# A bidirectional encoder layer with a Fourier and a Hyena branch: the weight rooms' pool laid out first, token 512's product in banks T for the later Fourier halves, its column parts on GpSimd

## The chip, the cores and the metric

The kernel runs on one core of one Trainium2 chip. The metric is the device time of one execution in microseconds (us). One core has a matrix engine (TensorE, PE in the profile, with its weight loads as PEld), VectorE (DVE), ScalarE (ACT), GpSimd (POOL) and SyncE (SP), which issues most transfers. The engines run side by side, each takes its own instructions strictly in order, and they wait for one another by semaphores. Working data lies in SBUF (on-chip memory of 128 partitions), products of TensorE in PSUM banks.

## What is computed

Two sequences (`x_prompt`, `x_sample`, below b = 0 and 1) of 1024 tokens and 1024 channels pass through the same layer. Cut to what matters:

```
xn = rmsnorm(x, g_pre);  p = xn @ w_in                      # 1024 -> 8192 columns
fv, fg, hv, hg, mg = split(p)
fz  = fftn(fv.reshape(B, L, 4, 256), axes=(1, 3), norm="ortho").real
y_f = (fz * silu(fg)) @ w_fourier_out                       # Fourier branch
v, x1, x2 = split(short_conv(hv, w_short), 3)
kf  = hyena_filters(...)                                    # 2 orders, two-sided, rfft
z = v;  for n, gate in enumerate((x1, x2)): z = gate * long_conv(z, kf[:, n], hyena_d[n])
y_h = (z * silu(hg)) @ w_hyena_out                          # Hyena branch
g_f, g_h = split(sigmoid(mg + b_merge))
out = x + rmsnorm((g_f * y_f + g_h * y_h) @ w_out, g_post)
```

The transforms are done as matrix products.

## The kernel before

**Values in two parts.** TensorE works on a rounded float32. Each operand is therefore kept as a high and a low part (`split`, line 168): a cast makes the high part (on ScalarE at line 171, on another engine at 173), a subtraction makes the low part (line 181). `mm3` multiplies high by high, high by low and low by high.

**Fourier phase** (`phase_fourier`). For each b, `norm` and then `xtile` for eight channel tiles k: TensorE transposes and scales the tile (`tpx`), ScalarE copies it to `xg`, and sums and differences of token j and token 1024 - j (`eo`: tokens folded around the middle) are split into `eh` and `el`, which lie in the pool `fe`. Token 512 is its own mirror and doesn't fit into the folds; it goes as a column of its own, split into two pieces of 128 x 2 in `x5`. Then come two halves of the channel groups, four in all, in the order (b, half) = (0,0), (0,1), (1,1), (1,0); weights are folded ahead of them on VectorE and GpSimd. In a half (`fourier_half`):

- `pfv`: the folded tokens by the weights, for the even folds (e = 0, 260 columns, into `ee`) and the odd ones (e = 1, into `oo`).
- `pfx`: the column of token 512 by the same weights, a product of 36 x 260 in sixteen matmuls. ScalarE copies it to `x5t` (line 416), VectorE makes its low part.
- `stage`: transforms along the tokens, `pse` and `pso`. In each `pse` of the even folds one matmul adds the alternating signs times `x5t`. ScalarE copies `pse` out (`sev`, line 439), VectorE joins it with `pso`.
- `pP` and `pQ`: transforms along the channels; VectorE makes `fA` and `fB`, which GpSimd's queue stores to `d_fz` (lines 491 and 492).

**PSUM.** Three tags share the eight banks: "mm" (four: `pfv`, `pin`, and `tpx` of b = 1), "X" (two: `pP`, `pQ`, half of the stages, and `pfx`) and "T" (two: `tpx` of b = 0, the other half of the stages, and `pft` of the filters).

**Main phase** (`phase_main`). First come sixteen filters. `filter_taps` makes products `pft`, exponentials on ScalarE (line 652, behind a table load) and norms `pn`; `filter_spectrum` makes the transform `pXf`. Thirty gate tiles (`spill_gate`, each an in-projection `inproj` of 48 `pin` matmuls) are spread among the filters as fill. Then `branches` and `phase_blocks` follow, which the change doesn't touch.

**Weight rooms.** A weight half comes in as `wr` (line 769); ScalarE casts it to its high part (773) and writes the negative of that (774), and a GpSimd transfer adds the source onto the negative, which leaves the low part (775). `rooms` gives such a pair of parts four places in turn: two buffers of `wh`/`wl` in the pool `wp`, the tile `draw` in `cp`, and the tile `draw2` in `stage2`, which is the pool m2 of `phase_main`. In `draw` and `draw2` both parts together are called `whl`.

**What sets the order.** The Tile scheduler orders the instructions of each engine by a simulated timeline, so that a change of buffers can also move instructions. Pools are laid out in SBUF in the order in which they are opened. With `reuse_waits="tile"`, a tile of a new pool waits only for the earlier tiles that lay in the same place. The Fourier phase opened px, fw, fe, fc, ff; in their place now come wp and xp, and above these the five pools of `phase_main`. Before the change m2 comes last of the five, and `draw2` lies over tiles of ff, the pool that the Fourier halves work in until their last instruction.

Of the kernel before, what the change touches and what calls it, by code (L numbers as in the profile page):

```python
# [161 lines left out]
class K:  # L162
# [171 lines left out]
    def xtile(self, b, k, px, fo):  # L334


        nc, a = self.nc, self.a
        if b == 0:
            xk = lambda m: self.xs[m][:, k * P:(k + 1) * P]
        else:  # L340
            xt = px.tile([P, 8, P], F32, tag="x", name=f"xk{b}_{k}", bufs=3)
            nc.sync.dma_start(xt, a[f"x{b}"].rearrange("(m p) c -> p m c", p=P)[:, :, k * P:(k + 1) * P])
            xk = lambda m: xt[:, m]
        xg = px.tile([P, L + 2], F32, tag="xg", name=f"xg{b}_{k}", bufs=2)
        nc.gpsimd.memset(xg[:, L:L + 2], 0.0)
        for n in range(2):
            tp = self.psum("mm", 4, "tpx") if b else self.psum("T", 2, "tpx")
            for q in range(4):
                m = 4 * n + q
                self.mm(tp[:, q * P:(q + 1) * P], xk(m), self.diag[:, m], True, True)  # L350
            nc.scalar.activation(xg[:, 512 * n:512 * n + 512], tp, AF.Copy, scale=self.gpre[:, k:k + 1])
        self.stored = nc.sync.dma_start(self.d_x[b][k], xg[:, 0:L])
        eo = px.tile([P, 2, 2, 256], F32, tag="eo", name="eo", bufs=2)
        fw = xg[:, 0:512].rearrange("p (a r) -> p r a", r=2)
        bw = xg[:, 1024:512:-1].rearrange("p (a r) -> p r a", r=2)
        self.add("dve", eo[:, 0], fw, bw)
        self.sub("pool" if b else "dve", eo[:, 1], fw, bw)
        self.split(fo["eh"][:, k], fo["el"][:, k], eo, "dve", "act")
        x5 = fo["x5"][:, k]
        mid = xg[:, 512:513].to_broadcast([P, 2])  # L360
        self.split(x5[:, b:b + 33:32], x5[:, 2 + b:35 + b:32], mid, "dve" if b else "pool", "dve" if b else "pool")


    def open_weights(self, pw):
# [26 lines left out]
    def fourier_half(self, b, half, W, fo, px, pf, begun={}):  # L391
# [7 lines left out]
        for e, (W_, n, X_) in enumerate(((WE, 260, EE), (WO, 256, OO))):  # L399
            for m in range(4):  # L400
                p = begun.get((e, m))
                if p is None:
                    p = self.psum("mm", 4, f"pfv{e}")
                    for k in range(8):
                        self.pfv(p, e, m, k, W, fo)
                self.split(X_[0][:, m], X_[1][:, m], p[:, :n], "dve", "act")
                if e == (b + half == 0):

                    if m == 0:
                        p5 = self.psum("X", 2, "pfx")[0:36, :260]  # L410
                    for k in (2 * m, 2 * m + 1):
                        for i in range(2):
                            self.mm(p5, fo["x5"][:, k], WE[i][:, k], k + i == 0, k + i == 8)
# [499 lines left out]
    def phase_main(self, nct=8, nb=NB, nf=16):  # L913
        tc, nc, a = self.tc, self.nc, self.a
        with ExitStack() as es:
            pool = lambda n: es.enter_context(tc.tile_pool(name=n, bufs=1, reuse_waits="tile"))
            mf, wa, wb, mi = pool("mf"), pool("wa"), pool("wb"), pool("mi")
            self.stage2 = pool("m2")
            self.turn, self.unsaved = 3, []
            ws = Rooms(wa, wb)  # L920
            self.load_x(0, range(4))
            self.hid = ws.tile([P, L], F32R, tag="q", name="hid", bufs=2)
            hid = ws.tile([P, L], F32, tag="q", name="hidr", bufs=2)
            nc.sync.dma_start(hid, self.d_h)
            nc.scalar.copy(self.hid, hid)
            self.sub("dve", self.hid[64:128], hid[64:128], self.hid[64:128])
            taps = self.filter_taps(0, 0, ws)
            self.load_x(0, range(4, 8))
            self.cfw0 = mf.tile([P, 4 * P], F32, name="cfw0")
            self.cfwd = mf.tile([P, 2, 12 * P], F32R, name="cfwd")  # L930
            nc.sync.dma_start(self.cfw0, a["c_fw0"])
            nc.gpsimd.tensor_copy(self.cfwd[:, 0, 0:1], self.xl[4][:, 0:1])
            nc.gpsimd.dma_start(self.cfwd, a["c_fwd"])
            for t, n in ((self.th, "c_th"), (self.wsh, "w_short"), (self.bm, "b_merge")):
                nc.sync.dma_start(t, a[n])
            plain = [(5, c) for c in range(8)] + [(6, c) for c in range(8)] + [(4, c) for c in range(NH)]
            fill = sorted([((2 * c + 1) / len(plain), t) for c, t in enumerate(plain)]
                          + [((2 * c + 1) / max(NF, 1), (0, c)) for c in range(NF)])
            fill = [t for _, t in fill]
            for i in range(nf):  # L940
                nxt = self.filter_taps((i + 1) % 2, (i + 1) // 2, ws) if i + 1 < nf else None
                gates = fill[i * len(fill) // nf:(i + 1) * len(fill) // nf]
                if i < nf - 1:
                    self.filter_spectrum(i % 2, i // 2, taps, ws)
                for sec, c in gates:
                    self.spill_gate(0, sec, c, ws)
                if i == nf - 1:
                    first = [self.conv(1 + n, 0, ws, "vx"[n], 0, True) for n in range(2)]
                    self.filter_spectrum(i % 2, i // 2, taps, ws)
                taps = nxt  # L950
                if i == 4:
                    self.cinv = mi.tile([P, 2, INVW], F32R, name="cinv")
                if 4 <= i < 12:
                    w = slice((i - 4) * INVW // 8, (i - 3) * INVW // 8)
                    with tc.issue_after(self.added.ins):
                        nc.gpsimd.dma_start(self.cinv[:, :, w], a["c_inv"][:, :, w])
            self.branches(nb, nct, ws, *first)
# [576 lines left out]
```

## Time and profile before

| what | value |
|---|---|
| median of 3 runs | 2417.44 us (2414.99 to 2423.45) |
| profiled execution | 2422.64 us |
| its span in the trace | 2420.8 us |
| mean granted TensorE clock | 0.993 |

Roughly, the Fourier phase takes the first 250 us and the filters with their fill last until about 660 us. "Busy" counts an instruction from its start to its end, and a matmul's end is modelled. A row of the timeline has a start, a duration, the engine, the line of the kernel, output and inputs by name, shape, the number of instructions that the row joins, and in brackets how long the engine stood idle ahead of it and what ended that.

### The profile page before, as it was taken

How to read it: one execution, taken by the hardware profiler on the slowest of the kernel's cores; microseconds unless marked ns; L12 is line 12 of the kernel's file. 1: busy time of each engine (PE TensorE's matmuls, PEld its weight loads, DVE VectorE, ACT ScalarE, POOL GpSimd, SP SyncE). 2: the span in 40 equal slices, each digit the busy share in tenths (PEclk: the TensorE clock that was granted, in tenths of full speed). 3: DMA queues.
4: the chain of work that ended last, by engine and by line, in shares of the span. 5: the costliest groups of instructions: out<-in, count | busy, mean ns of one | idle time of the engine just before them, and what ended most of it. 6: DMA issues, size and time to landing. Idle time of an engine off the chain costs nothing. (4 is left out here: it accounts for less than half of the span.)

```text
span 2420.8 us, 37131 instructions
## 1 busy us (share of the span) xinstructions
PE 2360.9 (98%) x13006; PEld 2050.1 (85%) x13006; DVE 1978.2 (82%) x3744; ACT 1147.2 (47%) x2140; POOL 460.4 (19%) x595
## 2 busy tenths in 40 slices
PE   7999899999999999999999999999999999999998
PEld 6998788888888888888888888888878888888786
DVE  7786888888638999999899999997666687777787
ACT  6546666667544444444223222333344465656543
POOL 3331111111132232321034444310000000101000
PEclk9999999999999999999999999999999999999999
DMA  7737687787788777665365666553546688888744
GB/s 250 231 105 233 178 226 214 212 227 214 193 234 246 222 222 210 187 182 191 126 208 174 219 210 205 175 178 122 204 165 226 214 290 262 261 272 234 214 158 155
DMA packets 265426, 499.37 MB, mean 206 GB/s; under 512 B 26694, under 2 KB 92455, under 8 KB 265112
## 3 DMA queue, kind: packets, MB, share of 16 engines
q1 hardware_dynamic: 220092, 380.27, 47.9%
q0 software_dynamic: 44960, 116.72, 18.9%
q8 instruction: 102, 1.67, 0.3%
q14 instruction: 84, 0.69, 0.1%
q10 hardware_dynamic: 188, 0.02, 0.0%
HBM read 333.59 MB, written 167.51 MB: 207 GB/s over the span
## 5 line engine op out<-in xcount | busy, mean ns | idle before, releaser
L194 PE MATMUL pin<-xh,wh 128*128 128x512 f32 x1024 | 400.9, 392 | 0.3 <-DMA wh<-d_w 0.3
L194 PE MATMUL pin<-xl,wh 128*128 128x512 f32 x1024 | 401.1, 392 | 0.0
L194 PE MATMUL pin<-xh,wl 128*128 128x512 f32 x1024 | 399.8, 392 | 1.3 <-DMA wl<-d_w 1.3
L194 PE MATMUL pin<-xh,whl 128*128 128x512 f32 x896 | 291.2, 396 | 8.1 <-DMA whl<-in_w_in 4.5
L194 PEld LDWEIGHTS pin<-xh,wl 128*128 128x128 f32 x1024 | 192.7, 188 | 37.4 <-DMA wl<-d_w 1.7
L194 PEld LDWEIGHTS pin<-xh,wh 128*128 128x128 f32 x1024 | 192.8, 189 | 35.7 <-DMA wh<-d_w 0.8
L194 PEld LDWEIGHTS pin<-xl,wh 128*128 128x128 f32 x1024 | 192.7, 188 | 34.7
L194 PEld LDWEIGHTS pin<-xh,whl 128*128 128x128 f32 x896 | 167.2, 189 | 42.1 <-DMA whl<-in_w_in 5.2
L194 PE MATMUL pT<-cinv,yh 128*128 128x256 f32 x1024 | 192.9, 283 | 2.3 <-ACT yh L171 2.3
L194 PE MATMUL pin<-xl,whl 128*128 128x512 f32 x448 | 177.6, 397 | 0.0
L194 PEld LDWEIGHTS pT<-cinv,yh 128*128 128x128 f32 x1024 | 165.4, 191 | 12.5 <-ACT yh L171 2.8
L194 PE MATMUL pX<-bh,cfwd 128*128 128x256 f32 x768 | 159.4, 287 | 1.0 <-ACT bh L171 1.0
L181 DVE TENSOR_TENSOR t<-pX,k 128x1024 f32<-128x1024 f32 x128 | 155.3, 1213 | 3.8 <-PE pX L194 3.0
L171 ACT CAST yh<-y 128x512 fp32r<-128x512 f32 x128 | 79.3, 620 | 160.2 <-DVE y L181 122.6
L194 PE MATMUL pT<-cinv,yl 128*128 128x256 f32 x512 | 145.6, 284 | 0.0
L171 ACT CAST bh<-b 128x512 fp32r<-128x512 f32 x144 | 89.0, 619 | 100.5 <-DVE b L181 61.6
L194 PEld LDWEIGHTS pX<-bh,cfwd 128*128 128x128 f32 x768 | 126.1, 192 | 4.7 <-ACT bh L171 1.4
L181 POOL TENSOR_TENSOR draw<-draw 128x256 f32<-128x256 f32 x96 | 90.3, 940 | 114.1 <-DMA draw<-in_w_out 41.6
L194 PE MATMUL pX<-bl,cfwd 128*128 128x256 f32 x384 | 110.0, 286 | 1.2 <-DVE bl L181 1.2
L181 DVE TENSOR_TENSOR bl<-b,bh 128x512 fp32r<-128x512 f32 x144 | 100.0, 700 | 12.7 <-ACT bh L171 12.5
L181 DVE TENSOR_TENSOR yl<-y,yh 128x512 fp32r<-128x512 f32 x128 | 92.4, 722 | 13.9 <-ACT yh L171 13.7
L177 DVE SCALAR_TENSOR_TENSOR x<-pin,wsh,x 128x512 f32<-128x512 f32 (+1 forms) x128 | 90.3, 739 | 12.0 <-ACT x L795 11.9
(372 smaller groups left out, 6049.6 us busy)
## 6 DMA issues: line engine op xcount, KB each, us to landing
k<-d_k SPq DMA_DIRECT2D x128, 512.0 KB, 4.5
wr<-in_w_in SPq DMA_DIRECT2D x136, 256.0 KB, 3.5
d_g<-gt SPq DMA_DIRECT2D x92, 256.0 KB, 3.2
d_k<-kt SPq DMA_DIRECT2D x128, 128.0 KB, 3.7
d_k<-kt SPq DMA_DIRECT2D x64, 256.0 KB, 3.8
fz<-d_g SPq DMA_DIRECT2D x64, 256.0 KB, 5.2
wl<-in_w_in POOLq DMA_DIRECT2D x56, 256.0 KB, 5.3
whl<-in_w_in POOLq DMA_DIRECT2D x56, 256.0 KB, 5.5
```

What stands on the lines that cost most here:

```text
L171: self.rounded = nc.scalar.copy(h, src)
L177: self.nc.vector.scalar_tensor_tensor(out, a, s, b, op0=op0, op1=op1)
L181: return e.tensor_tensor(out, a, b, op=op)
L194: return self.nc.tensor.matmul(out, lhsT, rhs, start=start, stop=stop, skip_group_check=shared)
```

## The change

It has three parts.

```diff
@@ xtile
         mid = xg[:, 512:513].to_broadcast([P, 2])
-        self.split(x5[:, b:b + 33:32], x5[:, 2 + b:35 + b:32], mid, "dve" if b else "pool", "dve" if b else "pool")
+        self.split(x5[:, b:b + 33:32], x5[:, 2 + b:35 + b:32], mid, "pool", "pool")
@@ fourier_half
                 if e == (b + half == 0):
 
                     if m == 0:
-                        p5 = self.psum("X", 2, "pfx")[0:36, :260]
+                        p5 = self.psum("T" if e == 0 else "X", 2, "pfx")[0:36, :260]
@@ phase_main
-            mf, wa, wb, mi = pool("mf"), pool("wa"), pool("wb"), pool("mi")
             self.stage2 = pool("m2")
+            wa, mf, wb, mi = pool("wa"), pool("mf"), pool("wb"), pool("mi")
```

- The two pieces of token 512 are made by GpSimd for b = 1 as well; for b = 0 GpSimd made them already.
- `pfx` runs with the even folds in all halves but the first, where it runs with the odd ones. In those three halves it now takes a bank of "T"; in the first it keeps one of "X".
- m2 is opened first, so that `draw2` lies just above wp and xp, where `el` lay in fe. wa comes next, and mf, with two constant tables of the transform (`cfw0`, `cfwd`), behind it.

TensorE's order is the same up to about 90 us and from about 660 us on. Between them it changes at these places, and the other engines' orders with it.

**TensorE, end of the last half** (`pQ` of the half's last products ahead, then the stages `pse` and `pso` of the even folds). Before:

```order
L194 MATMUL pQ<-px,chx 128x256
L194 MATMUL pfx<-we_2407,x_278 36x260
L194 MATMUL pfx<-we_2408,x_278 36x260
...
L194 MATMUL pse<-seq,ee_2491 128x258 x2
L194 MATMUL pse<-seq,ee_2492 128x258
L194 MATMUL pse<-seq,ee_2491 128x258 x2
L194 MATMUL pse<-seq,ee_2492 128x258
L194 MATMUL pse<-alt,x5t 128x258 x2
L194 MATMUL pso<-seq,ee_2491 128x258 x2
```

After:

```order
L194 MATMUL pQ<-px,chx 128x256
L194 MATMUL pfv_2701<-wo_2409,el 128x256
L194 MATMUL pse<-seq,ee_2491 128x258 x2
L194 MATMUL pse<-seq,ee_2492 128x258
L194 MATMUL pse<-seq,ee_2491 128x258 x2
L194 MATMUL pse<-seq,ee_2492 128x258
L194 MATMUL pse<-alt,x5t 128x258
L194 MATMUL pso<-seq,ee_2491 128x258 x2
```

The sixteen matmuls of `pfx` have left the place between `pQ` and `pse`; they now stand some 120 to 150 rows earlier, among the `pfv` of this half. The second `pse` of the even folds follows after the first `pso`. The two halves before it change in the same way.

**ScalarE, the same stretch** (`oo` and `pfv` belong to the last half; `hid`, `w3s`, `dec` and `ex` to the first filter; `whl_3590` is a weight half in the room `draw2`). Before:

```order
L171 CAST oo0_2493<-pfv1_2701 128x256
L925 CAST hid_2991<-hidr_2992 128x1024
L171 CAST w3s_2999<-w3_2996 128x256
L641 ACTIVATE dec_3002<-dec_3002 128x256
L416 CAST x5t_279<-pfx_2522 36x260
L652 ACT_TABLE_LOAD
L652 ACTIVATE ex_3009<-dec_3002,vec_68 128x256 x2
L652 ACTIVATE ex_3019<-dec_3002,vec_68 128x256 x2
L439 COPY sev_2753<-pse_2738 128x258
```

After:

```order
L171 CAST oo0_2493<-pfv1_2701 128x256
L773 CAST whl_3590<-wr_3591 128x512
L439 COPY sev_2753<-pse_2738 128x258
L774 ACTIVATE whl_3590<-whl_3590 128x512
L439 COPY sev_2778<-pse_2763 128x258
L171 CAST xh0_0_2971<-xl0_0_2972 128x1024
L171 CAST pp0_2736<-sst_2754 128x514
```

The cast of `whl_3590` stood 57 rows further down, among the exponentials of the second filter; it now follows the last `oo`, and its transfer (line 775) on GpSimd's queue has moved from behind the last four `d_fz` stores to ahead of them. The table load and the exponentials follow after four casts of the loaded sequence and all four `sev` copies of the even folds and the first odd one. On SyncE's queue the first loads of the sequence (`xl`) now come ahead of `hidr`, `w3` and `dec`.

**GpSimd, the token stage of b = 1** (`eo` is the difference of the folds for tile k, `x5` the pieces of token 512, `d_fz0` the stores of the half before). Before:

```order
L491 DMA d_fz0_0_93<-fA_1012 128x1024
L492 DMA d_fz0_1_94<-fB_1013 128x1024
L181 TENSOR_TENSOR eo_1750<-xg1_0_1735 128x512
L181 TENSOR_TENSOR eo_1774<-xg1_1_1759 128x512
L491 DMA d_fz0_2_95<-fA_1080 128x1024
L492 DMA d_fz0_3_96<-fB_1081 128x1024
```

After:

```order
L181 TENSOR_TENSOR eo_1750<-xg1_0_1735 128x512
L173 CAST x5_278<-xg1_0_1735 128x2
L181 TENSOR_TENSOR x5_278<-xg1_0_1735,x5_278 128x2
L491 DMA d_fz0_2_95<-fA_1080 128x1024
L492 DMA d_fz0_3_96<-fB_1081 128x1024
L345 MEMSET xg1_2_1783 128x2
L181 TENSOR_TENSOR eo_1774<-xg1_1_1759 128x512
L173 CAST x5_278<-xg1_1_1759 128x2
L181 TENSOR_TENSOR x5_278<-xg1_1_1759,x5_278 128x2
```

Each `eo` is now followed by the two instructions that make token 512's pieces, sixteen in all, which have left VectorE. On TensorE the `pfx` of the half that follows asks for the pieces of six of the eight tiles ahead of the first `pfv` of that half.

Between the filters the `pin` matmuls of the fill stand further ahead: TensorE reaches a filter's `pXf` after some 12 to 20 us more of such work than before, and after the same amount again at the last filter.

## The prediction

> **What bounds the kernel now.** I read the page first, then the list of TensorE's waits, then a table by stage, and then the timeline at the places that these three point to. The page:
>
> ```profile
> span 2420.8 us, 37131 instructions
> PE 2360.9 (98%) x13006; PEld 2050.1 (85%) x13006; DVE 1978.2 (82%) x3744; ACT 1147.2 (47%) x2140; POOL 460.4 (19%) x595
> ```
>
> TensorE is busy for 2360.9 of 2420.8 us, so all its idle time together is 60 us. A change that leaves its matmuls alone can gain only from those 60 us, and from stretches where it is busy at a lower granted clock. The change touches nothing before about 90 us and nothing after about 660 us. There, the table by stage (window, length, then busy time of TensorE, its weight loads, VectorE, ScalarE and GpSimd, the granted clock, the DMA share and GB/s):
>
> ```profile
> 97.50:130.60 33.10, 30.46 (x249) 29.99 (x248) 27.14 (x58) 19.77 (x33) 14.24 (x16) 0.95 0.74 247
> 197.20:212.20 15.00, 10.29 (x65) 8.70 (x64) 8.80 (x21) 9.00 (x16) 1.06 (x2) 0.89 0.81 282
> 249.65:269.16 19.51, 9.97 (x39) 7.50 (x37) 17.36 (x40) 9.56 (x20) 3.67 (x5) 0.74 0.60 159
> 300.00:360.00 60.00, 60.00 (x341) 52.55 (x340) 53.23 (x127) 42.57 (x93) 6.64 (x8) 1.00 0.83 225
> 540.00:600.00 60.00, 60.00 (x330) 52.06 (x329) 50.70 (x126) 41.15 (x89) 7.79 (x10) 1.00 0.82 228
> 600.00:660.00 60.00, 60.00 (x317) 51.51 (x317) 43.17 (x103) 35.60 (x76) 7.37 (x9) 1.00 0.72 191
> ```
>
> From 300 us TensorE never rests. The first three windows are the ones with something to win: 2.6, 4.7 and 9.5 us idle, at clocks of 0.95, 0.89 and 0.74. The waits between 180 and 300 us say what ends those idle times (line waited for, sum, times, longest):
>
> ```profile
> PE pin L194 <- DMA whl<-in_w_in: 4.5, 1, 4.5
> PE pin L194 <- ACT whl L773: 3.6, 1, 3.6
> PE pse L194 <- DVE x5t L181: 2.0, 1, 2.0
> PE pse L194 <- ACT sev L439: 1.6, 1, 1.6
> ```
>
> The upper two belong to the weight rooms, the lower two to token 512's product. Both are what the change moves.
>
> **Term A, the fourth weight room.** TensorE's timeline:
>
> ```profile
> 249.65 1.11 PE L194 MATMUL pft<-w3s,hid 128*128 128x256 f32 x8
> 252.16 0.74 PE L194 MATMUL pft<-w3s,hid 128*128 128x256 f32 x4 [1.40 <-DVE T L181]
> 256.51 0.79 PE L194 MATMUL pin<-xh,whl 128*128 128x512 f32 x1 [3.61 <-ACT whl L773]
> 257.10 0.63 PE L194 MATMUL pin<-xl,whl 128*128 128x512 f32 x1
> 257.53 0.63 PE L194 MATMUL pin<-xh,whl 128*128 128x512 f32 x1
> 263.11 1.22 PE L194 MATMUL pin<-xh,whl 128*128 128x512 f32 x2 [4.52 <-DMA whl<-in_w_in]
> 269.16 0.38 PE L664 MATMUL pn<-acc,ones 128*128 128x128 f32 x2
> 290.09 0.40 PE L194 MATMUL pin<-xl,wh 128*128 128x512 f32 x1
> ...
> 296.01 0.39 PE L194 MATMUL pin<-xh,wh 128*128 128x512 f32 x1
> ```
>
> From 249.65 to 269.16 lie 19.5 us. In them stand 12 pft and 24 pins. A pin takes 0.228 us (the last two rows stand 26 pins apart: 5.92 us over 26), so 24 take 5.5 us; 12 pft at about 0.118 (the slope in the first row: eight that end 1.11 us after they began, the last of them 0.28 long) take 1.4. That is 7.0 us of work and 12.5 us of loss: 9.5 us idle, and some 3 us in which the matmuls run slowly after the gap (257.10 to 257.53 is 0.43 us for one pin, against 0.228).
>
> Why the wait: the room draw2 lies over ff, which the last Fourier instruction still uses. ScalarE's cast into it came at 255.86, and the accumulating transfer behind it landed only before 263.11:
>
> ```profile
> 255.86 0.60 ACT L773 CAST whl<-wr 128x512 fp32r<-128x512 f32 x1
> 258.97 0.89 POOL L775 DMA_DIRECT2D whl<-in_w_in  x1 [6.50 <-ACT whl L774]
> whl<-in_w_in POOLq DMA_DIRECT2D x6, 256.0 KB, 5.0
> ```
>
> Laid out first, draw2 lies over el, whose last reader is a pfv matmul just ahead of the first pse (before 197.19 us in the trace of before). In the new order the cast stands some 60 rows earlier on ScalarE, right behind the last oo cast; the transfer, 5.0 us from issue to landing, can then be there some 40 us before TensorE asks for it. I take 12.5 less the 1.40 us wait for VectorE's T, which nothing here touches: **-11.1 us**. The ends are -8.1 (only 3.61 + 4.52 go, and the clock dips all the same, through another gap) and -12.5. The next room in turn becomes the tightest. In the order it has its transfer issued ahead of its first pin by the work of more than one gate, so I put no new wait there; term D holds that doubt.
>
> **Term B, token 512's product.** The end of the last Fourier half:
>
> ```profile
> 197.19 0.64 PE L194 MATMUL pse<-seq,ee 128*128 128x258 f32 x4
> 199.66 0.62 PE L194 MATMUL pQ<-qp,chan 128*128 128x256 f32 x3 [1.12 <-DVE fB L177]
> 200.48 2.07 PE L194 MATMUL pfx<-we,x 128*36 128x260 f32 x16
> 205.52 0.51 PE L194 MATMUL pse<-alt,x5t 128*128 128x258 f32 x2 [2.01 <-DVE x5t L181]
> 208.34 1.50 PE L194 MATMUL pse<-seq,ex 128*34 128x258 f32 x6 [1.58 <-ACT sev L439]
> 205.03 1.28 ACT L652 ACT_TABLE_LOAD   x1
> 206.32 1.70 ACT L652 ACTIVATE ex<-dec,vec 128x256 f32<-128x256 f32 x4
> 207.93 0.35 ACT L439 COPY sev<-pse 128x258 f32<-128x258 f32 x1
> ```
>
> pfx sits between pQ and pse, and its result must pass ScalarE and VectorE before the alternating product of pse can run: 2.01 us of nothing. The sev copy then stands behind a table load and four exponentials, 1.28 + 1.70 us: 1.58 us more. The window of 15.0 us holds 65 matmuls by the table, 4 of them pins: 61 at 0.12 (pfx's sixteen end 2.07 us after they began) and 4 at 0.228 are 8.2 us; 6.8 are lost. In the new order pfx stands inside the pfv pass, tens of matmuls ahead, and the sev copies come ahead of the table load. The 1.12 us wait for VectorE's fB is not of this part and stays: -6.8 + 1.1 = **-5.7 us**, ends -3.6 (2.01 + 1.58) and -6.8.
>
> The two other halves that change place have the same form, but with pfv, tpx and pse matmuls around them; their waits are part of term C.
>
> **Term C, the token stage of b=1.** The eight pairs of column pieces go from VectorE to GpSimd. What they cost on either engine (b=1 on VectorE between 100 and 140 us; b=0 on GpSimd between 20 and 60), and what GpSimd has there already:
>
> ```profile
> L173 DVE CAST x<-xg 128x2 fp32r<-128x2 f32 x8 | 5.2, 667 | 0.0
> L181 DVE TENSOR_TENSOR x<-xg,x 128x2 fp32r<-128x2 f32 x8 | 2.4, 316 | 0.1
> L173 POOL CAST x<-xg 128x2 fp32r<-128x2 f32 x8 | 9.1, 1136 | 13.0 <-ACT xg L351 13.0
> L181 POOL TENSOR_TENSOR x<-xg,x 128x2 fp32r<-128x2 f32 x8 | 3.6, 456 | 0.6
> L181 POOL TENSOR_TENSOR eo<-xg 128x512 f32<-128x512 f32 x8 | 15.2, 1910 | 8.2 <-ACT xg L351 6.5 <-DVE sst L445 1.5 <-POOL xg L345 0.2
> 30.65 4.93 POOL L173 CAST x<-xg 128x2 fp32r<-128x2 f32 x1 [1.53 <-ACT xg L351]
> 119.13 3.58 PE L194 MATMUL tpx<-dg,xk 128*128 128x128 f32 x16 [2.64 <-DMA xk<-in_x]
> ```
>
> VectorE is freed of 7.6 us in a window where it is busy 27.14 of 33.1. GpSimd gets 9.1 + 3.6 = 12.7 us beside its 15.2, so 27.9 of the some 29 us between its first eo (105.9) and its last (ended 135.1). That just fits; TensorE asks for the last el about 3.6 us after it is made. So GpSimd's lateness costs nothing up to 32.9 us, that is up to a mean of (32.9 - 15.2) / 8 = 2.2 us for a pair, against 1.59 in the rows. On the other side stands the 2.64 us wait for an xk tile, whose slot a faster stage hands back earlier. I take **-1.0 us**; the ends are -2.6 (all of that wait) and +3 (a pair takes 2.6 us; beyond it lies the second rival). What makes a piece urgent now is that pfx of the third half asks for six of the eight pieces in the middle of this stage, one after the other, and TensorE takes its matmuls in order.
>
> A rule that speaks against this part: the Trainium skill, "SBUF — State Buffer", Who interferes with whom, says that a GpSimd instruction that reads SBUF contends with a VectorE instruction that has two SBUF inputs, and that whoever holds the shared ports blocks the other for a whole instruction. The 4.93 us for two columns is of the kind it describes, while the mean of 1.14 us says that it strikes seldom. By the rows this term stays at -1.0; by the rule, were every piece blocked like that one, the time would be the second rival's.
>
> **Term D, new small waits.** pfx takes one of the two banks named T while the pfv pass runs, xl loads come ahead of hid and decay on the queue, and a room is next in turn. The trace of before has no such wait; the nearest is x5t's 2.01 us. Ends 0 and +4.0 (two such); I take one, **+2.0 us**.
>
> **The sum:** -11.1 - 5.7 - 1.0 + 2.0 = -15.8 us. The profiled execution took 2422.64 us (1.84 around its span), so a twin of it would take 2406.8. That execution lies 5.2 above the median of the three runs shown, 2417.44 (2414.99 to 2423.45); from that median the forecast is **2401.6 us**. All ends together give -21.9 (2395.5) and -4.7 (2412.7).
>
> **Rivals.**
> *Given back in the filter stage.* TensorE's fill, the pins, now runs some 18 us ahead of each filter's spectrum; the order of before 660 us ends where it ended. If VectorE paced that stage, it would reach the last filter when it does now, and TensorE would wait there. For: VectorE is busy 53.23 and 50.70 of 60 us in two of its windows. Against: even these leave 6.8 and 9.3 us in 60, some 50 in the six windows to 660, and 43.17 in the last of them. If a third to a half of the gain is kept, -5 to -8: 2409.4 to 2412.4.
>
> *Slower: GpSimd's pieces are held.* If each pair took 4.93 + 0.46 = 5.4 us, GpSimd would need 15.2 + 43.1 = 58.3 us against 32.9; pfx, then pfv, would wait 25.4 us for x5 and el. Less the 14.8 of A, B and D, that is +10.6: 2428.0. It eats the whole gain from a mean of (32.9 + 14.8 - 15.2) / 8 = 4.1 us for a pair, and is measurably slower (7.25 us more) from 5.0. For: one of the eight casts of b=0 took 4.93 us, more than half of the 9.1 that all took. Against: all eight together, with their subtractions, still took 12.7 us, 1.59 for a pair.
>
> *It does not do what it says.* draw2 may still be filled late, if the cast on ScalarE or its transfer on GpSimd's queue waits for something that comes only with the last half; then only B and C are left, and D eats part: -5.7 - 1.0 + 2.0 = -4.7, 2412.7; with a wait in B's place too, 2417.
>
> **How the numbers follow.** Forecast 0.66, given back 0.17, not as said 0.09, slower 0.08. A difference under 0.3% (7.25 us) is about what a measurement of this kernel cannot tell from none, so faster means below 2410.2: the forecast and half of the first rival, 0.74. Within 0.3% are the other half and the third rival, 0.18. Slower, 0.08. The range goes from the best end, 2395, to 2414, which takes in the forecast, its worst end and the first rival, and leaves out the slower rival and what of the third lies at 2417.
>
> **What would show it.** A: the waits for whl gone from the list, and a clock near 1 in the stretch that ends at the first pn behind pft. B: no wait for x5t; sev copies ahead of the table load. C: the pieces' mean on GpSimd near 1.1 and 0.5 us, TensorE's waits for x and el short. First rival: idle TensorE between 300 and 660 us, or a wait for VectorE before the last spectrum. I would be wrong if a room waits at another place for its transfer, or if pfx, which TensorE takes in order, holds the pfv behind it.

## The result

The changed kernel took 2405.58 us (median of 5 runs, 2402.20 to 2406.70), the kernel before 2417.44 (2414.99 to 2423.45). The ratio is 0.9936, with a 95% interval of 0.9921 to 0.9952: faster, by 0.5 to 0.8%. A second comparison (run 5 below) gave 2405.87 against 2419.33, ratio 0.9946 (0.9931 to 0.9960). The forecast was 2401.6, with a range of 2395 to 2414. So the direction was right and the time lay inside the range; of the 15.8 us of the sum, the medians show 11.9 and 13.5.

**The profile after.** The first two lines of the page:

```profile
span 2400.4 us, 37133 instructions
PE 2355.4 (98%) x13006; PEld 2048.0 (85%) x13006; DVE 1971.8 (82%) x3728; ACT 1143.9 (48%) x2140; POOL 478.2 (20%) x611
```

Idle TensorE is now 45 us instead of 60. The span fell by 20.4 us, more than the medians did, because the profiled execution of before was a long one. How much of this belongs to the change is read from instructions that both orders have at nearly the same place. These rows of TensorE's timeline are, in the kernel before, four `pin` matmuls of the fill, the start of the last half's odd stages behind them, and a transposition ahead of the branches:

```profile
211.14 0.78 PE L194 MATMUL pin<-xh,wh 128*128 128x512 f32 x2
211.76 0.63 PE L194 MATMUL pin<-xh,whl 128*128 128x512 f32 x2
212.22 0.90 PE L194 MATMUL pse<-seq,oo 128*128 128x258 f32 x6
776.11 1.04 PE L833 MATMUL tph<-ident,eo 128*128 128x128 f32 x8
```

The odd stages and the transposition in the changed kernel:

```profile
212.36 0.90 PE L194 MATMUL pse<-seq,oo 128*128 128x258 f32 x6
764.12 1.03 PE L833 MATMUL tph<-ident,eo 128*128 128x128 f32 x8
```

By these rows 0.1 us was lost up to the odd stages and 12.1 us won between the two. But the changed kernel runs its first `pin` only at 213.10, behind the start of the odd stages. Four pins at the prediction's 0.228 us are 0.9 us of work that the kernel before had already done there. With them on the same side of the row, the change loses 1.0 us up to the odd stages and wins 13.0 behind them. The rest of the 20.4 (8.4 us) comes later, where both kernels are in the same order: it is a difference between two executions, not an effect of the change. (From this transposition to the end, the fourteen profiled executions of this document took between 1636.3 us, the changed kernel, and 1644.7 us, the kernel before.)

TensorE's waits of the changed kernel between 180 and 300 us are a single line:

```profile
PE pQ L194 <- DVE fB L177: 4.6, 1, 4.6
```

All four of the waits shown of before are gone (4.5, 3.6, 2.0 and 1.6 us), and so is the 1.40 us wait of pft for VectorE's T. The one for fB, which was 1.1 us, has become 4.6. The timeline there, and the windows of 205 to 210 and 249.65 to 269.16 us (columns as before):

```profile
204.01 1.01 PE L194 MATMUL pQ<-qp,chan 128*128 128x256 f32 x3 [4.58 <-DVE fB L177]
205.68 1.49 PE L194 MATMUL pse<-seq,ee 128*128 128x258 f32 x6
206.97 0.42 PE L194 MATMUL pse<-alt,x5t 128*128 128x258 f32 x1
```

```profile
205.00:210.00 5.00, 5.00 (x26) 4.96 (x25) 2.74 (x8) 1.79 (x4) 1.94 (x3) 0.50 0.57 182
249.65:269.16 19.51, 19.51 (x100) 16.50 (x99) 14.37 (x31) 10.14 (x21) 4.58 (x7) 1.00 1.00 297
```

The alternating matmul follows its group at once: pfx no longer holds anything up. But behind the 4.58 us gap the granted clock is 0.50, and six pse matmuls take 1.49 us where they took 0.90 at full clock (212.36). In the second window, where 39 matmuls stood before, there are now 100, at a clock of 1.00. The room's part came, and the product's part was paid back on the spot.

**What fB waits for.** A half has two fA and two fB, which take turns in three buffers. So the second fB is written where the first fA lay, and has to wait until that fA is stored. VectorE's row, GpSimd's row with the issue of that store, and the first four loads of the sequence on SyncE's queue, in the changed kernel:

```profile
202.74 0.43 DVE L181 TENSOR_TENSOR fB<-pQ,fPm 128x258 f32<-128x258 f32 x1 [6.95 <-DMA d_fz<-fA]
192.01 0.57 POOL L491 DMA_DIRECT2D d_fz<-fA  x1 [0.19 <-issue]
190.31 0.92 SPq L731 DMA_DIRECT2D xl<-d_x  x2
191.29 0.46 SPq L731 DMA_DIRECT2D xl<-d_x  x1
205.96 0.32 SPq L731 DMA_DIRECT2D xl<-d_x  x1
```

And in the kernel before:

```profile
198.39 0.43 DVE L181 TENSOR_TENSOR fB<-pQ,fPm 128x258 f32<-128x258 f32 x1 [2.77 <-DMA d_fz<-fA]
191.16 0.56 POOL L491 DMA_DIRECT2D d_fz<-fA  x1
200.55 7.14 SPq L731 DMA_DIRECT2D xl<-d_x  x8
```

From the store's issue to fB it was 7.2 us before and is 10.7 now. The loads of xl moved from behind the load of hidr (200.55) to ahead of it (190.31), so that three of them, 512 KB each, have just been issued when the store goes out at 192.01. The fourth goes out at 205.96, when fB is already written, and so has no part in the wait. The DMA engines are busy for 0.96 of the 7.2 us and for 0.98 of the 10.7.

### The profile page after: what moved, and what is told of

It is laid out like the page before. It is cut to its first block, busy times and chain, and to the rows that moved or that the text cites. A ratio compares the mean times of both kernels' runs of the same rounds, so it can differ in the third digit from the quotient of the medians.

```text
span 2400.4 us, 37133 instructions
## 1 busy us (share of the span) xinstructions
PE 2355.4 (98%) x13006; PEld 2048.0 (85%) x13006; DVE 1971.8 (82%) x3728; ACT 1143.9 (48%) x2140; POOL 478.2 (20%) x611
## 5 line engine op out<-in xcount | busy, mean ns | idle before, releaser
L181 POOL TENSOR_TENSOR draw<-draw 128x256 f32<-128x256 f32 x96 | 96.4, 1004 | 109.9 <-DMA draw<-d_sh 38.2
L181 DVE TENSOR_TENSOR yl<-y,yh 128x512 fp32r<-128x512 f32 x128 | 89.7, 701 | 16.0 <-ACT yh L171 15.8
L194 PEld LDWEIGHTS pT<-cinv,yl 128*128 128x128 f32 x512 | 97.9, 191 | 1.9
```

Source lines behind the costliest of these rows:

```text
L181: return e.tensor_tensor(out, a, b, op=op)
L194: return self.nc.tensor.matmul(out, lhsT, rhs, start=start, stop=stop, skip_group_check=shared)
```

## The experiments

Theory 1: the room is worth its 11 to 12 us; the product's move frees 5 us, which are lost again because the loads of xl now go out first, delay the d_fz store and with it fB. Theory 2: the gain is shared among the parts, and fB's wait comes from the tighter order of the half. (The expectations speak of the four loads of xl that stand ahead of hidr; the rows above show three of them under way beside the store.) All times are medians, with the ratio to the kernel before on the same chip and its 95% interval.

**1. The rooms alone.**

```diff
-            mf, wa, wb, mi = pool("mf"), pool("wa"), pool("wb"), pool("mi")
             self.stage2 = pool("m2")
+            wa, mf, wb, mi = pool("wa"), pool("mf"), pool("wb"), pool("mi")
```

> Only the pool order is changed; token 512's pieces and product stay as before. Theory 1 (the whole gain is the fourth weight room; the rest gives nothing): about 12 us faster than before, 2405, no wait for whl between 180 and 300 us, and still waits of about 2.0 and 1.6 us for x5t and sev. Theory 2 (the parts share the gain, the room 8 and the product 4): 2409 to 2410.

2409.91 us, ratio 0.9965 (0.9954 to 0.9977): 9.5 us faster, between the 12 of theory 1 and the 8 of theory 2. The waits between 80 and 300 us:

```profile
PE pse L194 <- DVE x5t L181: 2.6, 1, 2.6
PE pQ L194 <- DVE fB L177: 1.7, 1, 1.7
PE pse L194 <- ACT sev L439: 1.6, 1, 1.6
```

whl is gone, x5t and sev are there, as theory 1 had it. In this execution TensorE falls behind in two places. The odd stages start at 214.21, 2.0 us later than in the kernel before. And between 270 and 660 us TensorE is idle for 4.8 us, in waits such as these (265 to 720 us):

```profile
PE pn L664 <- DVE acc L181: 3.2, 4, 1.4
PE pXf L194 <- ACT kt L710: 1.2, 2, 1.0
```

That is the first rival of the prediction, in small: with the pins ahead, VectorE paces part of the filter stage. This profiled execution took 2414.22 us, 4.3 more than the median, so its waits cannot simply be laid on the median.

**2. The product alone.**

```diff
-                        p5 = self.psum("X", 2, "pfx")[0:36, :260]
+                        p5 = self.psum("T" if e == 0 else "X", 2, "pfx")[0:36, :260]
```

> Only pfx takes the banks T in the three later halves. Theory 1 (the four loads of xl that come ahead of hidr hold back the d_fz stores, and fB waits for these): within 3 us of before; no wait for x5t, and a wait of 3 us or more of pQ for fB in its place; the waits for whl stay at about 4.5 and 3.6 us. Theory 2 (the product is worth its share): 4 to 6 us faster than before.

2419.93 us, ratio 0.9998 (0.9989 to 1.0008): no gain, as theory 1 had it. The waits between 80 and 300 us begin with the exchange:

```profile
PE pQ L194 <- DVE fB L177: 4.6, 1, 4.6
PE pin L194 <- DMA whl<-in_w_in: 4.6, 1, 4.6
PE pin L194 <- ACT whl L773: 3.6, 1, 3.6
```

In this kernel the loads of xl come ahead of hidr, though nothing but pfx's bank was changed; in that of run 1 they don't. It is the product's move that turns the queue around.

**3. The pieces alone.**

```diff
-        self.split(..., mid, "dve" if b else "pool", "dve" if b else "pool")
+        self.split(..., mid, "pool", "pool")
```

> Only the pieces of token 512 go to GpSimd for b = 1. Both theories: within 2 us of before, the eight casts at a mean under 1 us. The rival of the prediction (pieces held on GpSimd) would show casts of 3 us and more and a time above before by several us.

2421.86 us, ratio 1.0006 (0.9994 to 1.0017): no difference that can be told (the medians lie 2.4 us apart, a little over the 2 us expected). The changed kernel's profile (GpSimd, 97 to 142 us, by form) shows why the slower rival didn't come:

```profile
L181 POOL TENSOR_TENSOR eo<-xg 128x512 f32<-128x512 f32 x8 | 17.0, 2119 | 13.2 <-ACT xg L351 8.4 <-ACT fPm L481 2.3 <-DVE sst L445 1.8
L173 POOL CAST x<-xg 128x2 fp32r<-128x2 f32 x8 | 3.8, 477 | 0.0
L181 POOL TENSOR_TENSOR x<-xg,x 128x2 fp32r<-128x2 f32 x8 | 3.4, 425 | 0.4
```

A pair takes 0.9 us, not the 1.59 of the b = 0 rows, and far from the 4.1 at which the gain would have been gone.

**4. The changed kernel with hidr loaded first.**

```diff
-            self.load_x(0, range(4))
             self.hid = ws.tile([P, L], F32R, tag="q", name="hid", bufs=2)
             hid = ws.tile([P, L], F32, tag="q", name="hidr", bufs=2)
-            nc.sync.dma_start(hid, self.d_h)
+            loaded = nc.sync.dma_start(hid, self.d_h)
+            with tc.issue_after(loaded.ins):
+                self.load_x(0, range(4))
```

> The changed kernel, but the first four loads of xl stand behind the load of hidr on SyncE's queue, as in the kernel before. Theory 1: the d_fz stores land earlier, pQ's wait for fB falls from 4.6 to about 1 us, and the time to about 2400, 4 to 6 us below the changed kernel's 2405.6. Theory 2 (fB waits because the half's own order is tighter, whatever the queue does): the wait stays above 3 us and the time within 2 us of 2405.6.

2400.84 us, ratio 0.9930 (0.9918 to 0.9943). VectorE's, SyncE's and TensorE's rows:

```profile
199.94 0.43 DVE L181 TENSOR_TENSOR fB<-pQ,fPm 128x258 f32<-128x258 f32 x1 [3.23 <-DMA d_fz<-fA]
200.75 2.12 SPq L731 DMA_DIRECT2D xl<-d_x  x4
201.21 0.63 PE L194 MATMUL pQ<-qp,chan 128*128 128x256 f32 x3 [0.87 <-DVE fB L177]
206.83 0.89 PE L194 MATMUL pse<-seq,oo 128*128 128x258 f32 x6
760.78 1.03 PE L833 MATMUL tph<-ident,eo 128*128 128x128 f32 x8
```

The wait falls from 4.58 to 0.87 us, and the odd stages start at 206.83 in place of 212.36: 5.5 us (3.1 against the second execution of the changed kernel, in run 5). Runs 2 and 7, and runs 11 and 12, are the same comparison in other kernels: with the loads of xl first the wait is 4.6 and 4.3 us, with them later 0.9 and 0.7. That settles the cause of fB's wait, and the second half of theory 2 falls. What it is worth in the whole time is less sure: the median is some 5 us below the changed kernel's, but the ratios, 0.9930 here and 0.9936 and 0.9946 there, have intervals that overlap.

**5. The changed kernel again.**

> The changed kernel once more, on the same chip as the next three. About 2405 to 2406, with a wait of 4 to 5 us of pQ for fB.

2405.87 us; the wait of pQ for fB is 4.49 us, and the transposition starts at 761.69. Here the odd stages began at 209.92, 2.4 us earlier than in the first execution of the same kernel, so the part up to that point varies by some two us between executions. Against the kernel before, 2.3 us are won up to there and 14.4 up to the transposition, so 12.1 between them again (1.4 and 13.0 with the four pins on the same side).

**6. Rooms and pieces, without the product.** The diff of run 2 undone in the changed kernel.

> The changed kernel with pfx back in the banks X. Theory 1 (the product's move gives nothing while the loads of xl come first): within 3 us of the changed kernel. Theory 2 (it gives part of the gain, in the filter stage, although the end of the Fourier phase shows none): 3 to 6 us slower than the changed kernel, as the room alone was (2409.9), with idle time of TensorE between 270 and 660 us.

2407.99 us, ratio 0.9954 (0.9939 to 0.9969); the changed kernel beside it 0.9946 (0.9931 to 0.9960). The 2.1 us are within the intervals, as theory 1 had it, and TensorE was not idle between 270 and 660 us. This kernel differs from that of run 1 by the pieces alone, and yet it has none of run 1's 4.8 us of idle time. The two ratios (0.9954 and 0.9965) overlap in their intervals. With one profile of each, it is not shown whether the pieces' order or the execution makes that difference.

**7. Product and hidr first, with the old rooms.** The diffs of runs 2 and 4 on the kernel before.

> The kernel before with pfx in the banks T and the first four loads of xl behind the load of hidr; rooms and pieces as before. Theory 1 (the lost term B was lost to these loads): about 5 us faster than before where the product alone was within 1 us, pQ's wait for fB near 1 us, the whl waits of 4.5 and 3.6 us still there. Theory 2: within 2 us of before.

2417.72 us, ratio 0.9992 (0.9979 to 1.0005). A miss: 5 us were expected. The waits of TensorE, 80 to 300 us, of which fB is only 0.9:

```profile
PE pin L194 <- DMA whl<-in_w_in: 4.4, 1, 4.4
PE pin L194 <- ACT whl L773: 3.6, 1, 3.6
...
PE pin L194 <- DMA wl<-in_w_in: 2.1, 1, 2.1
PE pft L194 <- DVE T L181: 1.4, 1, 1.4
...
PE pQ L194 <- DVE fB L177: 0.9, 1, 0.9
```

The gain at fB was there, and was lost again at the rooms. The odd stages start at 206.76 instead of 212.22, but the transposition at 776.76 instead of 776.11. Between the two, TensorE is idle for 12.6 us instead of 9.6: it waits 2.1 us for a wl that cost nothing before, and for whl and T as long as before. The rest of the loss is the four pins and slower matmuls (a clock of 0.91 between 230 and 250 us, where it was 1.00). The product's move, with the queue put right, pays only if the room is mended too.

**8. Hidr first, without the pieces.** The diff of run 4 in the changed kernel, that of run 3 undone.

> The changed kernel with hidr first and the pieces of token 512 back on VectorE. If the pieces give nothing, within 2 us of the kernel with hidr first (2400.8); if VectorE's 7.6 us decide the token stage, 3 us or more above it, with longer waits of TensorE between 100 and 140 us.

2401.26 us, ratio 0.9933 (0.9915 to 0.9952), against 2400.84 with the pieces (ratio 0.9930): no gain from them that can be told.

**9. m2 first, the other pools in their old order.**

```diff
-            mf, wa, wb, mi = pool("mf"), pool("wa"), pool("wb"), pool("mi")
             self.stage2 = pool("m2")
+            mf, wa, wb, mi = pool("mf"), pool("wa"), pool("wb"), pool("mi")
```

> The kernel before with m2 opened first and the other four pools in their old order (mf, wa, wb, mi). If the place of draw2 alone carries the gain: no waits for whl, and within 3 us of the room order of the change (2409.9). If moving mf behind wa is part of it: several us of the gain missing, with new waits of TensorE between 200 and 300 us, since the loads that feed the filters then stand in another order (hidr comes behind the eight loads of xl).

2400.07 us, ratio 0.9921 (0.9900 to 0.9941): about 10 us below run 1, and the two kernels differ only in that mf stays ahead of wa. A miss: neither case of the expectation had that. TensorE's waits between 80 and 300 us have no whl. With runs 4 and 8 this is the fastest of all, some 5 us below the changed kernel's medians, though its interval still overlaps those of both comparisons of the changed kernel. Against run 1's profiled execution, 13.6 us are won up to the transposition (759.50 for 773.12), more than half of them up to the odd stages (206.06 for 214.21). hidr now goes out at 248.54 us, so hid, w3s and dec no longer stand ahead of x5t's copy on ScalarE. The rows of ScalarE and TensorE:

```profile
202.56 0.37 ACT L416 CAST x5t<-pfx 36x260 fp32r<-36x260 f32 x1 [0.96 <-PE pfx L194]
200.46 2.06 PE L194 MATMUL pfx<-we,x 128*36 128x260 f32 x16
203.44 0.51 PE L194 MATMUL pse<-alt,x5t 128*128 128x258 f32 x2
```

pfx stands where it stood, and yet nothing waits for x5t. In the kernel before, the copy came at 204.66, 2.1 us after pfx had ended, behind this row:

```profile
204.34 0.42 ACT L641 ACTIVATE dec<-dec 128x256 f32<-128x256 f32 x1 [1.70 <-DMA dec<-in_filt_decay]
```

So pfx's old place need not cost a wait. What made x5t late in the kernel before was a load for the first filter that ScalarE waited for ahead of the copy.

**10. mf behind wa, m2 last.**

```diff
-            mf, wa, wb, mi = pool("mf"), pool("wa"), pool("wb"), pool("mi")
+            wa, mf, wb, mi = pool("wa"), pool("mf"), pool("wb"), pool("mi")
             self.stage2 = pool("m2")
```

> The kernel before with mf opened behind wa, and m2 still last. If the place of draw2 carries the gain: within 2 us of before, and the whl waits of 4.5 and 3.6 us still there.

2420.36 us, ratio 1.0007 (0.9998 to 1.0017): no gain. TensorE's waits between 80 and 300 us still begin with the room:

```profile
PE pin L194 <- DMA whl<-in_w_in: 4.3, 1, 4.3
PE pin L194 <- ACT whl L773: 3.6, 1, 3.6
```

With runs 1 and 9, where m2 is opened first and these waits are gone, this shows that the room's place carries the gain.

**11. Run 9 with product and pieces.**

> m2 first with the other pools in their old order, and the product and the pieces as in the change. With m2 first alone x5t's wait was gone although pfx kept its place, since hid, w3s and dec no longer stand ahead of x5t's copy on ScalarE. If that is the cause, moving pfx adds nothing, and the loads of xl, which come first again, hold back fB: a wait of 4 to 5 us of pQ for fB, and 4 to 6 us slower than m2 first alone (2400.1), about 2405. If pfx's move has a worth of its own: 2400 or below.

2406.77 us, ratio 0.9948 (0.9931 to 0.9965); pQ waits 4.3 us for fB, as the first reading had it. On top of run 9, product and pieces together cost some 6 us by the medians and 5.0 by the transposition (764.46 for 759.50), though the intervals of the two ratios overlap a little.

**12. Run 11 with the loads of xl behind that of cfw0.**

```diff
+            self.cfw0 = mf.tile([P, 4 * P], F32, name="cfw0")
+            loaded = nc.sync.dma_start(self.cfw0, a["c_fw0"])
+            with tc.issue_after(loaded.ins):
+                self.load_x(0, range(4))
...
+            with tc.issue_after(loaded.ins):
+                self.load_x(0, range(4, 8))
```

> The same with the loads of xl behind the load of cfw0, which goes out only when the last pfv are done, as with m2 first alone. If the copy's place on ScalarE was the cause of x5t's wait: within 2 us of m2 first alone (2400.1), pQ's wait for fB near 1 us. If pfx's move has a worth of its own, 3 us or more below it, 2397.

2408.91 us, ratio 0.9960 (0.9946 to 0.9975): a miss. The odd stages start at 206.70, as early as in run 9 (206.06), and fB costs 0.7 us. Then the gain runs out in the filter stage, in waits such as these (270 to 720 us):

```profile
PE pn L664 <- DVE acc L181: 2.2, 3, 1.1
PE pXf L194 <- DVE b L181: 1.2, 2, 0.6
```

```profile
270.00:660.00 390.00, 384.16 (x2111) 329.99 (x2110) 326.50 (x791) 261.53 (x574) 49.53 (x61) 1.00 0.77 207
```

TensorE is idle for 5.8 of these 390 us; in run 9 it is idle for 0.1, and in the changed kernel for none. From the odd stages to the transposition this execution takes 561.8 us, that of run 9 553.4. So the move of pfx shows no worth of its own here, but the question is not cleanly answered, since another loss came in. Why this order meets VectorE's pace and that of run 9 doesn't was not tried and stays open.

## Why the prediction was right, and where it was not

- **Term A, the room (-11.1; measured -12.1 between the two rows in both profiles of the changed kernel, -13.0 with the four pins on the same side).** Right in cause: whl's waits and the low clock behind them are gone, runs 1, 9 and 10 show that draw2's place does it, and no next room took over. Its size was put 1.9 us too low, mostly because the 1.40 us wait for VectorE's T, "which nothing here touches", went as well.
- **Term B, the product (-5.7; measured with C and D together +0.1 and -2.3 at the odd stages, or +1.0 and -1.4 with the four pins, where the three terms said -4.7).** The step that failed is the sentence "The 1.12 us wait for VectorE's fB is not of this part and stays". The change of SyncE's order was written down ahead of the prediction (xl ahead of hidr), but what these loads hold up was not followed: fB's wait became 4.58 us, with a clock of 0.50 behind it. Run 4 puts the queue back, and the odd stages start 5.5 and 3.1 us earlier than in the two profiles of the changed kernel. A second step failed too: x5t's 2.01 us was charged to pfx's place. In run 9 pfx keeps its place and the wait is gone, because the first filter's loads no longer stand ahead of the copy on ScalarE. The step on sev was right: its copies come ahead of the table load, and its wait is gone.
- **Term C, the pieces (-1.0).** No gain that can be told, by runs 3 and 8. In the changed profile xk's 2.6 us wait shrinks to 0.5, and waits for qp (1.0), sev ahead of pfx (0.9), xg (0.7) and fB (0.5) come in its place. The Trainium skill's rule on the shared ports ("SBUF — State Buffer", Who interferes with whom), by which every piece could be held for a whole instruction, does not decide here: the mean of the eight casts is 0.48 us, and the longest takes 0.66.
- **Term D, new small waits (+2.0).** One came. The term names the loads of xl, but not the store and fB that they hold up. The wait was 3.5 us longer than the one it grew from, not counting the slower clock behind it.
- **The rivals.** *Given back in the filter stage*: not in the changed kernel (389.96 of 390 us busy between 270 and 660), but it is a real mechanism: runs 1 and 12 show it, with 4.8 and 5.8 us of idle time. *Held pieces*: did not come; 0.9 us for a pair. *Does not do what it says*: true of the product's part in its effect, not of the room.

So the time came out some 4 us above the forecast because A was right; B was lost nearly whole. That it came so near is partly luck: A won 1.9 us more than it was put at, which made up for part of B.

## What to carry to other kernels

When a change reorders a program, list the transfers that change places as carefully as the waits that go: a load that starts earlier can take its time from a store that somebody waits for. Before charging a wait to the product that comes late, look at what its reader's engine had in front of it. And a gain ahead of another wait on the same path can be worth nothing until that wait is mended too (run 7), so parts are to be measured together and apart.

## What was not expected of the hardware

A 512 KB store that went out just behind three loads of 512 KB, the first of them 1.7 us ahead of it, held its buffer until 10.7 us after its issue. With the loads later it was 7.2 us (7.0 in run 4: issue at 192.96, fB at 199.94). GpSimd issued the store and SyncE the loads, so two issuing engines did not keep them apart. And the same two-column cast on GpSimd that took 1.14 us in the mean, with a longest of 4.93, in the stage of b = 0, took 0.48 in that of b = 1.
